# Head pairs that wait for less: new start conditions for the units of an RWKV-7 / mLSTM / mixture-of-experts block, with three key buffers and overlapping token halves

## The chip, the cores and the metric

The kernel runs on one core of a Trainium2 chip. The metric is the device time of one execution in microseconds; lower is better. The time before is the median of three runs, and one more execution was taken with the hardware profiler.

The engines are named as in the profile: PE is TensorE (matmul), PEld its weight loads, DVE is VectorE, ACT is ScalarE, POOL is GpSimd, SP is SyncE, which here issues nearly all DMAs. Each engine works through its own queue in order and waits at semaphores.

## What is computed

One layer of a streaming encoder block on 1024 tokens of width 1024, in float32:

```python
mod = jax.nn.silu(c) @ ada_w[l] + ada_b[l]
sh_m, sc_m, g_m, sh_f, sc_f, g_f = jnp.split(mod, 6, axis=-1)
h = modulate(rms_norm(x, mix_norm_w[l]), sh_m, sc_m)
proj = h @ w_in[l]
y_r = rwkv7_group(proj[..., :RWKV_COLS], ...)    # 8 heads of 64
y_m = mlstm_group(proj[..., RWKV_COLS:], ...)    # 4 heads, keys 64, values 128
y = jnp.concatenate([y_r, y_m], axis=-1) @ w_out[l]
x = x + g_m[:, None, :] * y
h = modulate(rms_norm(x, ffn_norm_w[l]), sh_f, sc_f)
y = hier_moe(h, ...)                             # 32 experts in 4 groups, two per token
x = x + g_f[:, None, :] * y
return rms_norm(x, final_norm_w)
```

The RWKV-7 group is a recurrence over the tokens, for each head with a 64x64 state (decay `w_t`, a rank-one correction `sa b`, a rank-one update `v k`):

```python
def step(state, inp):
    r_t, w_t, k_t, v_t, kk_t, b_t = inp
    sa = jnp.einsum('bhij,bhj->bhi', state, -kk_t)
    state = (state * w_t[:, :, None, :] + sa[..., None] * b_t[:, :, None, :]
             + v_t[..., None] * k_t[:, :, None, :])
    return state, jnp.einsum('bhij,bhj->bhi', state, r_t)
```

The mLSTM group is a chunked linear attention with stabilised exponential gates and a carried matrix state; its output is normalised per head and gated.

## The kernel before

**Stages.** After a short start (the first modulation vectors, four early products) come the mixer, the output projection w_out, the routing and the experts. In the mixer the tokens are in two halves of 512 (`SH`). For each half the normalised input lies transposed in SBUF (`hT`, one buffer), and the columns of `w_in` are taken 128 at a time.

**Jobs.** A `Job` is one such product: 128 columns by 512 tokens, 8 steps over the depth of 1024, each step three matmuls (`mm3`: high by high, high by low, low by high part of split operands), so 24 matmuls of 512 columns into one of two PSUM banks, the lanes. These are the lane matmuls (lines 411 to 413). `fetcher` loads a job's weights (SP, line 425), `splitter` makes the two parts (ACT, then DVE or POOL, lines 440 and 441), `products` issues the matmuls, and the job's `out` reads the lane. A half has one job for the two low-rank inputs `wd` and `ad`, one for `gd`, three per unit (key `k`, receptance `r`, value `v`), twelve for mLSTM and one for its gates. The eight jobs of w_out for each half run through the same lanes (`out_jobs`). `ORDER` is a string per half: a digit stands for the three jobs of that unit, `g` for `gd`, `m` for an mLSTM job.

**Units.** A `Unit` is a pair of RWKV heads in one half: units 0 to 3 in the first, 4 to 7 in the second. Its stages, each a generator:
- `unit_prep`: decays and rates from `wd`, the norm of the keys (`nrm`, a few small DVE steps, then transposed back by PE at line 735), decay-weighted operands `AR` and `BK`, the in-chunk products `G`
- `unit_rest`: transposes the values
- `unit_solve`: inverts 16x16 triangular blocks on DVE. `G` goes to DRAM, is read back as `N16`, the result goes to DRAM as an image and is read back as `X16` and `D16` (SP, line 850; a short D or X in the profile)
- `unit_levels`: puts the blocks together to the 64x64 inverse (PE from line 865)
- `unit_scan`: eight steps in series with the state, each a ping-pong of small matmuls and DVE or POOL operations
- `unit_post`: group norm, bonus, gate, transposition (lines 973 to 998); the result goes to `yTd` in DRAM

**The planner.** PE's order is written out when the kernel is built. `Weave` runs a set of generators in a simulated time. A generator yields a pair (PE time used, latency until it goes on) or a condition; the first ready one in a fixed order of priority is taken, with `products` last, so that lane matmuls fill whatever is left. The latencies stand in the table `LAT`, in microseconds as its author assumed them. A wrong assumption is paid on the chip: PE takes its instructions in that order and stands if an operand isn't there. The other engines' orders come from the compiler's scheduler, with priorities that the generators set.

A unit starts under this condition:

```python
yield lambda: u.jobs[0].done and u.h in b.wd and b.prepped >= n and b.scanned >= n - 1 and b.posted >= n - 1
```

`prepped`, `scanned` and `posted` count the units that have passed the stage: unit n waits until unit n-1 is prepared and unit n-2 is scanned and through post. Keys and receptances have two buffers; their jobs wait for `prepped >= n - 1`.

**The other streams.** `misc` runs in series: the gates of half 0, the remaining four modulation vectors (`ada_rest`, which multiplies rows of `ada_w` into an accumulator on DVE, line 248), `router_x` (64 transposes of x), `h_second` (the second half's `hT`, after all jobs of the first), mLSTM chunks 0 to 3, the gates of half 1, and, once all mLSTM jobs of the half are done, chunks 4 to 7. An mLSTM chunk is 128 tokens: loads, exponentials, scores, numerators (lines 1200 and 1201), the new state (line 1210), and then a tail: norm on ACT and DVE, scaling on POOL, transposition on PE (line 1238), gate, store. `outs` reads y for w_out: the first half's (`y_first`) when all units are prepared and no job of the second half runs, the second half's (`y_second`) after the jobs of w_out's first half. w_out takes its steps over the depth in an order in which unit 7 comes last.

Of the kernel before, what the change touches and what calls it, by code (L numbers as in the profile page):

```python
# [8 lines left out]
F32 = mybir.dt.float32  # L9
# [9 lines left out]
P = 128  # L19
# [19 lines left out]
def f1(n):  # L39
    return n / 2400.0  # L40


LAT = dict(split=3.56, split2=1.5, fetch=4.0, job=1.5, prep0=2.5, prep1=3.06, prep2=11.15, v=0.11, lev1=1.06, lev2=0.35, lev3=1.09, lev4=0.9,
           s1=0.63, s2=0.85, s3=0.51, post1=12.11, post2=5.87, vcm=2.41, gates=20.0, d1=5.0, d2=2.14, d3=0.8, d4=13.0, solve=34.0,
           ada=1.85, x1=18.0, x2=2.5, yk=5.0, lx=2.13, e3=13.7, e4=2.08, rows=12.0, p_prep=-3000, p_rest=0, p_lev=10000, p_scan=300,
           p_post=0, p_gates=0, p_ada=-1000, p_rx=0, p_h=-1000, p_chunk=-1000, p_split=-300, p_prod=0, p_fin=-3000, p_fetch=0, p_y=10000, yk1=1.91,
           u0=0.0)

# [5 lines left out]
class Block:  # L54
# [188 lines left out]
    def ada_k(self, pool, acc, lo, n, tag, bufs, k):  # L243
        nc = self.nc
        a = self.a['ada_w']
        w = pool.tile([P, n], F32, tag=tag + "w", name="ada_w", bufs=bufs)
        nc.sync.dma_start(w, bass.AP(tensor=a.tensor, offset=a.offset + k * P * 6 * D + lo, ap=[[6 * D, P], [1, n]]))
        nc.vector.scalar_tensor_tensor(acc, w, self.csil[:, k:k + 1], acc, op0=ALU.mult, op1=ALU.add)

    def ada_rest(self, pool):  # L250
# [4 lines left out]
        for q in range(4):  # L255
# [4 lines left out]
            for k in range(KD):  # L260
                self.ada_k(pool, acc, lo, D, "adr", 3, k)
                yield 0, LAT['ada']
# [22 lines left out]
    def normed(self, pool, t):  # L285

        nc = self.nc
        j = pool.tile([P, D], BF16, tag="junk", name="junk", bufs=1)
# [74 lines left out]
    def y_first(self, hpool, pool):  # L363
# [3 lines left out]
        for k in self.h_order:  # L367
            t = pool.tile([P, SH], F32, tag="kr"[k % 2], name="yraw", bufs=2)
# [5 lines left out]
    def y_stage(self, pool):  # L374
# [4 lines left out]
        for tag, n in (("k", 2), ("r", 2), ("kk", 1), ("aa", 1), ("cs", 1)):  # L379
            for _ in range(n):  # L380
# [4 lines left out]
                t = self.staged[k] = pool.tile([P, SH], F32, tag=tag, name="yraw", bufs=2 if tag in ("k", "r", "cs") else 1)[:, 0:n_]  # L385
# [83 lines left out]
    def lora_wd(self, pool, h, ps):  # L469
        wd = pool.tile([P, SH], F32, tag="wdad", name="wdad", bufs=2)  # L470
# [4 lines left out]
    def lora_gd(self, pool, h, ps):  # L475
        gd = pool.tile([P, SH], F32, tag="gd", name="gd", bufs=2)
# [104 lines left out]
def products(b):  # L581
# [3 lines left out]
    while b.jobs or b.fetched or b.split or b.running:  # L585
# [8 lines left out]
        for i_, k in enumerate(b.h_order):  # L594
# [8 lines left out]
            yield 3 * f1(512), 0  # L603
# [41 lines left out]
def unit_jobs(u):  # L645
# [4 lines left out]
    def out(name, mu_i):  # L650
        def f(ps):
# [6 lines left out]
            else:  # L658
                t = u.tile(name, [SH], bufs=2)
# [4 lines left out]
    u.jobs = [Job(b, h, 512 + p * P, out("k", 4 + p), when=lambda: b.prepped >= n - 1),  # L664
              Job(b, h, p * P, out("r", p), when=lambda: b.prepped >= n - 1),
# [3 lines left out]
def unit(u):  # L669
    b, n = u.b, u.no  # L670
    w = b.weave
    yield lambda: u.jobs[0].done and u.h in b.wd and b.prepped >= n and b.scanned >= n - 1 and b.posted >= n - 1
# [4 lines left out]
    b.prepped = n + 1  # L677
    t0 = w.now
    yield 'rest'
    yield from unit_rest(u)  # L680
    b.rested = n + 1
    yield lambda: b.levelled >= n
    with b.tc.high_priority(offset=20000):
        unit_solve(u)
# [467 lines left out]
def mlstm_chunk(self, i, pool):  # L1152
# [37 lines left out]
    yield 2 * f32(P), LAT['d3']  # L1190
    C = self.C
    sm = pool.tile([P, 4, 4], F32, tag="msm", name="msm", bufs=2)
    dn, rd, ss, t = (sm[:, j] for j in range(4))
    v4 = lambda x: x.rearrange("p (a e) -> p e a", e=2)
# [11 lines left out]
    if i < NT - 1:  # L1206
# [8 lines left out]
        yield 4 * f32(129), 0  # L1215
    jk = E[:, 0]
# [740 lines left out]
def build(ctx, tc, aps):  # L1957
# [44 lines left out]
    if True:  # L2002
# [4 lines left out]
        for h in range(2):  # L2007
            Job(b, h, 1536, lambda ps, h=h: b.lora_wd(sp, h, ps))
# [3 lines left out]
            for c in ORDER[h]:  # L2012
                if c == "g":
                    Job(b, h, 1536 + P, lambda ps, h=h: b.lora_gd(sp, h, ps))
# [13 lines left out]
        def misc():  # L2028
# [7 lines left out]
            with tc.tile_pool(name="lx", bufs=1, **right) as pool:  # L2036
                yield 'rx'
                yield from router_x(b, pool)
# [3 lines left out]
            with tc.tile_pool(name="at0", bufs=1, **right) as pool:  # L2042
                mlstm_chunks(b, pool)
                for i in range(4):
                    yield 'chunk'
                    yield from mlstm_chunk(b, i, pool)
            misc_done.append(0)
# [4 lines left out]
            with tc.tile_pool(name="at1", bufs=1, **right) as pool:  # L2052
                mlstm_chunks(b, pool)
                for i in range(4, 8):
                    yield 'chunk'
                    yield from mlstm_chunk(b, i, pool)
                misc_done.append(1)
# [66 lines left out]
ORDER = ["0g123mmmmmmmmmmmm", "0gm1mmmmm2mmmmmm3"]  # L2124
# [34 lines left out]
```

## Time and profile before

| | |
|---|---|
| median of 3 runs | 1334.13 us (1328.01 to 1370.47) |
| profiled execution | 1337.15 us |
| its span, first to last instruction | 1335.4 us |
| mean granted TensorE clock | 0.906 |
| PE busy | 1159.8 us, 87% |
| PE weight loads busy | 837.5 us, 63% |
| DVE, ACT, POOL busy | 941.6, 529.5, 389.0 us |

The clock is the share of full speed that the chip granted TensorE, a mean over two levels, 1.0 (2.4 GHz) and 0.5 (1.2 GHz). The span lies inside the profiled execution's own time. Stages by time from the span's start: up to some 62 us the start, then the mixer with its units, from 748.57 us the jobs of w_out, then routing, and the experts from about 945 us to the end.

### The profile page before, as it was taken

What the parts mean: (1) busy time and instruction counts of PE and PEld (TensorE: products, weight loads), DVE (VectorE), ACT (ScalarE), POOL (GpSimd) and SP (SyncE); (2) the same over time, 40 slices, a digit from 0 to 9 for tenths busy, and PEclk for the clock granted to TensorE, in tenths of its full rate; (3) what the DMA queues carried; (4) which work ended last, traced back from release to release, by engine and by line L of the source; (5) the groups of instructions that cost most, each with busy time, mean ns of one, the idle gap of its engine ahead of it and who ended that gap; (6) DMA issues with size and microseconds to landing.
All of it is one profiled execution on the core that took longest, in us unless ns stands there. A gap on an engine that the chain in (4) does not pass through costs nothing. (4 is left out here: it accounts for less than half of the span.)

```text
span 1335.4 us, 21827 instructions
## 1 busy us (share of the span) xinstructions
PE 1159.8 (87%) x7807; PEld 837.5 (63%) x7807; DVE 941.6 (71%) x2024; ACT 529.5 (40%) x1021; POOL 389.0 (29%) x464
## 2 busy tenths in 40 slices
PE   3876889898898998999988799996799998999893
PEld 2654656677566777676756666775566665565553
DVE  6778868876567787757837744743788887777766
ACT  5433222233333442232423332545455655544444
POOL 4613122312232423322324233434222222222212
PEclk8978889878999997999988889879799999999997
DMA  9435545356524443131452454598499989999974
GB/s 318 118 96 164 156 139 183 123 143 189 178 70 99 112 111 79 47 98 49 111 157 70 132 171 123 164 317 282 156 313 318 295 284 295 305 320 332 319 267 170
DMA packets 251935, 246.16 MB, mean 184 GB/s; under 512 B 55064, under 2 KB 190362, under 8 KB 251824
## 3 DMA queue, kind: packets, MB, share of 16 engines
q1 hardware_dynamic: 243504, 228.43, 54.9%
q0 software_dynamic: 8320, 16.31, 5.2%
q8 instruction: 62, 1.02, 0.3%
q14 instruction: 49, 0.40, 0.1%
HBM read 212.13 MB, written 44.74 MB: 192 GB/s over the span
## 5 line engine op out<-in xcount | busy, mean ns | idle before, releaser
L411 PE MATMUL lane<-hTh,whi 128*128 128x512 f32 (+1 forms) x544 | 252.7, 465 | 3.9 <-DVE u L1026 3.5
L412 PE MATMUL lane<-hTl,whi 128*128 128x512 f32 (+1 forms) x544 | 228.0, 419 | 4.2 <-POOL hTl L361 2.6
L413 PE MATMUL lane<-hTh,wlo 128*128 128x512 f32 (+1 forms) x544 | 226.9, 417 | 0.0
L440 ACT CAST whi<-wraw 128x512 fp32r<-128x512 f32 x140 | 84.5, 609 | 267.8 <-PE lane L412 210.0
L441 POOL TENSOR_TENSOR wlo<-wraw,whi 128x512 fp32r<-128x512 f32 (+1 forms) x70 | 92.3, 1320 | 199.9 <-ACT whi L440 173.2
L1667 PE MATMUL yd<-wd,a 128*112 128x512 f32 x256 | 122.0, 615 | 15.8 <-DMA wd<-in_moe_w_down_dram 13.2
L411 PEld LDWEIGHTS lane<-hTh,whi 128*128 128x128 f32 (+1 forms) x544 | 108.9, 200 | 35.8 <-issue 8.0
L413 PEld LDWEIGHTS lane<-hTh,wlo 128*128 128x128 f32 (+1 forms) x544 | 109.3, 201 | 27.6 <-DVE wlo L441 0.3
L412 PEld LDWEIGHTS lane<-hTl,whi 128*128 128x128 f32 (+1 forms) x544 | 110.0, 202 | 22.0 <-POOL hTl L361 3.4
L1590 DVE TENSOR_TENSOR wl<-wa,wh 128x1024 fp32r<-128x1024 f32 x62 | 75.5, 1225 | 40.9 <-ACT wh L1589 39.4
L411 PE MATMUL lane<-wh,xh 128*112 128x512 f32 x256 | 103.8, 405 | 0.0
L413 PE MATMUL lane<-wh,xl 128*112 128x512 f32 x256 | 101.3, 396 | 0.0
L412 PE MATMUL lane<-wl,xh 128*112 128x512 f32 x256 | 101.2, 395 | 0.0
L1694 POOL DMA_INDIRECT x2d<-ys,idx x30 | 44.9, 1496 | 152.8 <-DVE ys L1678 143.9
L1667 PEld LDWEIGHTS yd<-wd,a 128*112 128x112 f32 x256 | 43.9, 184 | 70.7 <-issue 45.1
L1590 DVE TENSOR_TENSOR wl<-wb,wh 128x1024 fp32r<-128x1024 f32 x62 | 76.3, 1230 | 14.0 <-ACT wh L1589 13.8
L1589 ACT CAST wh<-wa 128x1024 fp32r<-128x1024 f32 x64 | 66.8, 1049 | 45.9 <-PE lane L413 17.8
L1589 ACT CAST wh<-wb 128x1024 fp32r<-128x1024 f32 x64 | 67.3, 1051 | 20.1 <-DMA wb<-in_moe_w_up_dram 10.8
L441 DVE TENSOR_TENSOR wlo<-wraw,whi 128x512 fp32r<-128x512 f32 (+1 forms) x70 | 52.3, 747 | 30.3 <-ACT whi L440 17.2
L935 POOL TENSOR_SCALAR sW<-st,WT 128x64 f32<-128x64 f32 x56 | 33.5, 600 | 137.4 <-DVE st L948 118.9
L1596 POOL DMA_INDIRECT xt<-xad,idx x32 | 34.7, 1084 | 121.3 <-PE tp L1620 96.4
L1678 DVE SCALAR_TENSOR_TENSOR ys<-yd,tb,gf 112x512 f32<-112x512 f32 x64 | 44.9, 742 | 14.1 <-PE yd L1667 13.9
(522 smaller groups left out, 2457.8 us busy)
## 6 DMA issues: line engine op xcount, KB each, us to landing
wd<-in_moe_w_down_dram SPq DMA_DIRECT2D x64, 512.0 KB
wraw<-in_w_in_dram SPq DMA_DIRECT2D x104, 256.0 KB
ada_w<-in_ada_w_dram SPq DMA_DIRECT2D x32, 512.0 KB
wa<-in_moe_w_gate_dram SPq DMA_DIRECT2D x32, 512.0 KB
wa<-in_moe_w_up_dram SPq DMA_DIRECT2D x32, 512.0 KB
wb<-in_moe_w_gate_dram SPq DMA_DIRECT2D x32, 512.0 KB
wb<-in_moe_w_up_dram SPq DMA_DIRECT2D x32, 512.0 KB
ada_w<-in_ada_w_dram SPq DMA_DIRECT2D x32, 256.0 KB
```

Source lines behind the costliest of these rows:

```text
L411: nc.tensor.matmul(ps, l[0], r[0], start=first, stop=False)
L412: nc.tensor.matmul(ps, l[0], r[1], start=False, stop=False)
L413: self.mark = nc.tensor.matmul(ps, l[1], r[0], start=False, stop=last)
L440: nc.scalar.copy(hi, raw)
L441: (nc.gpsimd if q else nc.vector).tensor_tensor(lo, raw, hi.bitcast(F32), op=ALU.subtract)
L935: nc.gpsimd.tensor_scalar(sW, st, WT[:, c:c + 1], None, op0=ALU.mult)
L1589: nc.scalar.copy(h, src)
L1590: (engs[n] if engs else nc.vector).tensor_tensor(l, src, h.bitcast(F32), op=ALU.subtract)
L1596: return self.nc.gpsimd.indirect_dma_start(out=self.xts[e % 3], out_offset=None, in_=self.xad[:], in_offset=bass.IndirectOffsetOnAxis(ap=s ...
L1667: self.nc.tensor.matmul(y[:, b], a[:, i], d[:, i, b * 512:b * 512 + 512], start=(i == 0), stop=(i == 1))
L1678: nc.vector.scalar_tensor_tensor(ys[:, bs], py[b], cw, self.gf[0:SL, bs], op0=ALU.mult, op1=ALU.mult)
L1694: self.nc.gpsimd.indirect_dma_start(out=self.x2d[:], out_offset=bass.IndirectOffsetOnAxis(ap=oi, axis=0), in_=ys, in_offset=None, bounds_c ...
```

## The change

- A unit waits for the scan of unit n-2 as before, no longer for its post. The condition on post moves behind `unit_prep`, ahead of `unit_rest`.
- If the levels of unit n-1 are already placed when prep ends, the solve is emitted there, ahead of `unit_rest`; else after the rest, as before, and then the assumed latency of the solve counts from its emission.
- Keys and receptances have three buffers (`KR`), and their jobs wait for `prepped >= n - 2`. To make room, `wdad` and `gd` have one buffer, whose jobs in the second half wait until unit 3 is prepared and through post; the scratch tile of the norm shares a buffer with `hv`. The tiles staged for w_out's second half use the third buffers.
- The planner assumes 4.5 for 3.06 us (norm factors), 28 for 34 (solve), 0.693 for 0.64 us (three lane matmuls).
- `ada_rest` loads and multiplies halves of 512 columns, with six buffers instead of three twice as wide.
- The tail of an mLSTM chunk is a stream of its own, so that the next chunk's loads, exponentials and scores can be placed before it ends. The numerators of chunk i wait until the tail of chunk i-1 is through.
- `router_x` comes after chunks 0 to 3 instead of before `h_second`.
- In the second half all units' jobs come ahead of the mLSTM jobs, as in the first.

```diff
-           ... prep1=3.06 ... solve=34.0,
-           ada=1.85, ...
+           ... prep1=4.5 ... solve=28.0,
+           ada=1.6, ...
+PROD = 0.693
+KR = 3
...
             for k in range(KD):
-                self.ada_k(pool, acc, lo, D, "adr", 3, k)
-                yield 0, LAT['ada']
+                for v in range(2):
+                    self.ada_k(pool, acc[:, v * SH:(v + 1) * SH], lo + v * SH, SH, "adr", 6, k)
+                    yield 0, LAT['ada']
...
-        j = pool.tile([P, D], BF16, tag="junk", name="junk", bufs=1)
+        j = pool.tile([P, SH], F32, tag="hv", name="junk", bufs=1).bitcast(BF16)
...
-            t = pool.tile([P, SH], F32, tag="kr"[k % 2], name="yraw", bufs=2)
+            t = pool.tile([P, SH], F32, tag="kr"[k % 2], name="yraw", bufs=KR)
...
-        for tag, n in (("k", 2), ("r", 2), ("kk", 1), ("aa", 1), ("cs", 1)):
+        for tag, n in (("k", KR), ("r", KR), ("kk", 1)):
...
-        wd = pool.tile([P, SH], F32, tag="wdad", name="wdad", bufs=2)
+        wd = pool.tile([P, SH], F32, tag="wdad", name="wdad", bufs=1)
...
-        gd = pool.tile([P, SH], F32, tag="gd", name="gd", bufs=2)
+        gd = pool.tile([P, SH], F32, tag="gd", name="gd", bufs=1)
...
-            yield 3 * f1(512), 0
+            yield PROD, 0
...
-                t = u.tile(name, [SH], bufs=2)
+                t = u.tile(name, [SH], bufs=KR)
...
-    u.jobs = [Job(b, h, 512 + p * P, out("k", 4 + p), when=lambda: b.prepped >= n - 1),
-              Job(b, h, p * P, out("r", p), when=lambda: b.prepped >= n - 1),
+    u.jobs = [Job(b, h, 512 + p * P, out("k", 4 + p), when=lambda: b.prepped >= n - KR + 1),
+              Job(b, h, p * P, out("r", p), when=lambda: b.prepped >= n - KR + 1),
...
-    yield lambda: u.jobs[0].done and u.h in b.wd and b.prepped >= n and b.scanned >= n - 1 and b.posted >= n - 1
+    yield lambda: u.jobs[0].done and u.h in b.wd and b.prepped >= n and b.scanned >= n - 1
...
     b.prepped = n + 1
+    early = b.levelled >= n
+    if early:
+        with b.tc.high_priority(offset=20000):
+            unit_solve(u)
     t0 = w.now
+    yield lambda: b.posted >= n - 1
     yield 'rest'
     yield from unit_rest(u)
     b.rested = n + 1
-    yield lambda: b.levelled >= n
-    with b.tc.high_priority(offset=20000):
-        unit_solve(u)
+    if not early:
+        yield lambda: b.levelled >= n
+        with b.tc.high_priority(offset=20000):
+            unit_solve(u)
+        t0 = w.now
     yield 0, max(0.0, t0 + LAT['solve'] - w.now)
...
     yield 2 * f32(P), LAT['d3']
+    yield lambda: self.chunks == i
     C = self.C
...
         self.C = Cn
         yield 4 * f32(129), 0
+    self.weave.spawn(mlstm_tail(self, i, pool, E, nv, sm, og))
+
+
+def mlstm_tail(self, i, pool, E, nv, sm, og):
...
+    yield 'chunk'
     jk = E[:, 0]
...
-            Job(b, h, 1536, lambda ps, h=h: b.lora_wd(sp, h, ps))
+            Job(b, h, 1536, lambda ps, h=h: b.lora_wd(sp, h, ps), when=lambda h=h: b.prepped >= 4 * h)
...
-                    Job(b, h, 1536 + P, lambda ps, h=h: b.lora_gd(sp, h, ps))
+                    Job(b, h, 1536 + P, lambda ps, h=h: b.lora_gd(sp, h, ps), when=lambda h=h: b.posted >= 4 * h)
...
-            with tc.tile_pool(name="lx", bufs=1, **right) as pool:
-                yield 'rx'
-                yield from router_x(b, pool)
             with tc.tile_pool(name="h1", bufs=1, **right) as pool:
...
                     yield from mlstm_chunk(b, i, pool)
+                yield lambda: b.chunks == 4
+            with tc.tile_pool(name="lx", bufs=1, **right) as pool:
+                yield 'rx'
+                yield from router_x(b, pool)
             misc_done.append(0)
...
                     yield from mlstm_chunk(b, i, pool)
+                yield lambda: b.chunks == 8
...
-ORDER = ["0g123mmmmmmmmmmmm", "0gm1mmmmm2mmmmmm3"]
+ORDER = ["0g123mmmmmmmmmmmm", "0g123mmmmmmmmmmmm"]
```

## Rows read from the trace of the kernel before

**Rows 1.** The page: busy time of each engine over the span

```profile
PE 1159.8 (87%) x7807; PEld 837.5 (63%) x7807; DVE 941.6 (71%) x2024; ACT 529.5 (40%) x1021; POOL 389.0 (29%) x464
```

**Rows 2.** Stages: window, length, busy us (x) of PE, PEld, DVE, ACT, POOL; clock, DMA

```profile
62.00:849.00 787.00, 695.84 (x5849) 517.34 (x5847) 553.52 (x1438) 257.77 (x567) 227.49 (x299) 0.89 0.44 122
62.00:236.00 174.00, 136.73 (x1173) 101.43 (x1172) 138.03 (x283) 49.07 (x88) 46.50 (x60) 0.84 0.49 145
236.00:405.00 169.00, 152.59 (x1378) 112.68 (x1376) 114.12 (x321) 53.30 (x101) 41.82 (x56) 0.89 0.48 141
540.00:670.00 130.00, 123.03 (x1024) 89.52 (x1023) 95.72 (x256) 44.89 (x89) 37.09 (x59) 0.99 0.32 78
670.00:804.00 134.00, 115.75 (x1035) 85.03 (x1035) 75.62 (x228) 42.69 (x120) 43.39 (x49) 0.85 0.47 132
945.00:1335.00 390.00, 350.08 (x1408) 229.46 (x1408) 300.73 (x365) 199.27 (x285) 89.42 (x67) 0.96 0.88 288
```

**Rows 3.** Timeline of PE around 670: start, us, instruction, [idle before <-releaser]

```profile
668.77 0.39 PE L412 MATMUL lane<-hTl,whi 128*128 128x512 f32 x1
669.00 0.39 PE L413 MATMUL lane<-hTh,wlo 128*128 128x512 f32 x1
674.69 1.08 PE L865 MATMUL tp<-D,G 32*32 32x32 f32 x64 [5.30 <-DMA D<-img]
...
676.29 0.63 PE L412 MATMUL lane<-hTl,whi 128*128 128x512 f32 x1
676.72 0.63 PE L413 MATMUL lane<-hTh,wlo 128*128 128x512 f32 x1
```

**Rows 4.** Waits of PE: who for whom, us in total, times, longest

```profile
PE tp L735 <- DVE nrm L195: 20.1, 4, 12.5
```

**Rows 5.** Timelines of ACT and DVE: units 0, 2 and 7

```profile
171.50 0.69 ACT L449 ACTIVATE k<-lane,omu 128x512 f32<-128x512 f32 x1
...
216.97 0.28 DVE L948 SCALAR_TENSOR_TENSOR stf<-pp,WT,sW 128x64 f32<-128x64 f32 x1
...
243.31 0.59 ACT L998 COPY yt<-tp 128x512 f32<-128x512 f32 x1
249.29 0.69 ACT L711 ACTIVATE sw<-tp,phalf 128x512 f32<-128x512 f32 x1 [5.39 <-PE tp L714]
...
695.93 0.68 ACT L449 ACTIVATE k<-lane,omu 128x512 f32<-128x512 f32 x1
698.35 0.72 ACT L705 ACTIVATE sq<-k,pcol 128x512 f32<-128x512 f32 x1 [1.73 <-POOL k L454]
```

**Rows 6.** Timelines of SP and PE: the solve's reads and unit 7's levels

```profile
667.13 0.54 SPq L850 DMA_DIRECT2D D<-img  x1
...
770.18 0.53 SPq L850 DMA_DIRECT2D D<-img  x1
...
784.80 0.75 PE L865 MATMUL tp<-D,G 32*32 32x32 f32 x64 [0.33 <-DVE pB L1182]
```

**Rows 7.** Timeline of PE: numerators and tails of chunks 4 and 7, lane jobs

```profile
703.19 0.49 PE L1200 MATMUL tp<-vt,pB 128*128 128x129 f32 x2
...
730.62 0.60 PE L1238 MATMUL tp<-ident,mnv 128*128 128x128 f32 x4
...
748.57 0.78 PE L411 MATMUL lane<-hTh,whi 128*128 128x512 f32 x1
...
823.11 0.49 PE L1200 MATMUL tp<-vt,pB 128*128 128x129 f32 x2
...
842.50 0.60 PE L1238 MATMUL tp<-ident,mnv 128*128 128x128 f32 x4
...
849.62 0.47 PE L411 MATMUL lane<-hTh,whi 128*128 128x512 f32 x1
```

**Rows 8.** Lines 248 and 227: ns min/median/max; what DVE waited for

```profile
L248 DVE SCALAR_TENSOR_TENSOR ada_rest<-ada_w,csil,ada_rest x32: 1262/1284/1993, 118.6 to 250.1; 128x1024 f32<-128x1024 f32 x32
...
  DMA ada_w<-in_ada_w_dram: 9.4, 9
...
L227 DVE SCALAR_TENSOR_TENSOR ada_acc<-ada_w,csil,ada_acc x20: 735/750/1750, 19.4 to 48.6; 128x512 f32<-128x512 f32 x20
```

More of the change, by code (lines that the diff above doesn't have):

```diff
@@ L40, in f1 @@
     return n / 2400.0
-LAT = dict(split=3.56, split2=1.5, fetch=4.0, job=1.5, prep0=2.5, prep1=3.06, prep2=11.15, v=0.11, lev1=1.06, lev2=0.35, lev3=1.09, lev4=0.9,
-           s1=0.63, s2=0.85, s3=0.51, post1=12.11, post2=5.87, vcm=2.41, gates=20.0, d1=5.0, d2=2.14, d3=0.8, d4=13.0, solve=34.0,
-           ada=1.85, x1=18.0, x2=2.5, yk=5.0, lx=2.13, e3=13.7, e4=2.08, rows=12.0, p_prep=-3000, p_rest=0, p_lev=10000, p_scan=300,
+LAT = dict(split=3.56, split2=1.5, fetch=4.0, job=1.5, prep0=2.5, prep1=4.5, prep2=11.15, v=0.11, lev1=1.06, lev2=0.35, lev3=1.09, lev4=0.9,
+           s1=0.63, s2=0.85, s3=0.51, post1=12.11, post2=5.87, vcm=2.41, gates=20.0, d1=5.0, d2=2.14, d3=0.8, d4=13.0, solve=28.0,
+           ada=1.6, x1=18.0, x2=2.5, yk=5.0, lx=2.13, e3=13.7, e4=2.08, rows=12.0, p_prep=-3000, p_rest=0, p_lev=10000, p_scan=300,
            p_post=0, p_gates=0, p_ada=-1000, p_rx=0, p_h=-1000, p_chunk=-1000, p_split=-300, p_prod=0, p_fin=-3000, p_fetch=0, p_y=10000, yk1=1.91,
            u0=0.0)
+PROD = 0.693
+KR = 3
 def bcast_rows(ap, n, parts=P):
@@ L384, in y_stage @@
                 n_ = SH if k < 4 else SH - P
-                t = self.staged[k] = pool.tile([P, SH], F32, tag=tag, name="yraw", bufs=2 if tag in ("k", "r", "cs") else 1)[:, 0:n_]
+                t = self.staged[k] = pool.tile([P, SH], F32, tag=tag, name="yraw", bufs=n)[:, 0:n_]
                 self.nc.sync.dma_start(t, self.yTd[k * P:(k + 1) * P, SH:SH + n_])
@@ L1190, in mlstm_chunk @@
     yield 2 * f32(P), LAT['d3']
+    yield lambda: self.chunks == i
     C = self.C
     sm = pool.tile([P, 4, 4], F32, tag="msm", name="msm", bufs=2)
-    dn, rd, ss, t = (sm[:, j] for j in range(4))
-    v4 = lambda x: x.rearrange("p (a e) -> p e a", e=2)
     nv = []
@@ L1215, in mlstm_chunk @@
         yield 4 * f32(129), 0
+    self.weave.spawn(mlstm_tail(self, i, pool, E, nv, sm, og))
+def mlstm_tail(self, i, pool, E, nv, sm, og):
+    nc = self.nc
+    tok = self.tok
+    ts_ = slice(i * P, (i + 1) * P)
+    dn, rd, ss, t = (sm[:, j] for j in range(4))
+    v4 = lambda x: x.rearrange("p (a e) -> p e a", e=2)
+    yield 'chunk'
     jk = E[:, 0]
```

## Prediction

> **What bounds the kernel now.** I read the page's engine line first, then a table of stages, then who waits for whom, then short timelines. TensorE (PE) is busy for 87% of the span, DVE for 71%, ACT and POOL for less [rows 1]. In the table of stages [rows 2] the expert part (945 to 1335) is full and the change does not touch it: whatever the mixer (62 to 849) saves or loses moves that part as a block. In the mixer PE is the bound, but not a full one. Its first row has 695.84 us of busy PE in 787, so 91 us are idle. The granted clock adds to that: a mean of 0.89 between the two levels 1.0 and 0.5 is half speed for 2 x 0.11 of the time, 173 us at 1.2 GHz. A lane matmul (the large product of the input projection) follows the one before it after 0.23 us at 2.4 GHz and after 0.43 us at 1.2 GHz [rows 3], so half speed costs up to half of those 173 us, 87 us. The reader should see two poor stages, 62 to 236 and 670 to 804, and one that shows what is possible, 540 to 670 (7 us idle, clock 0.99). Low clock and gaps go together: the 5.30 us wait that ends at 674.69 is followed by lane matmuls at 0.43 us [rows 3].
>
> The gaps have two kinds of cause. PE runs a fixed order, worked out by a planner that assumes latencies. Where the planner assumed too little, PE stands at the instruction: for the transposed norm factors 20.1 us in 4 waits, the longest 12.5 [rows 4]. And where units start late, the work that could fill the gaps has already been used.
>
> **The change, part by part.** All terms are against the profiled execution: 1337.15 us, of which the span is 1335.4 us; it lies 3 us over the median of the runs, 1334.13.
>
> *The start of a unit.* Unit 0's scan wrote its last state at 216.97, its post copied its result at 243.31, and unit 2's first activation came at 249.29; unit 3 stands to unit 1 in the same way [rows 5]. So the old condition on post is what holds the third unit, by some 26 us, and the new one releases it. It is not the third buffer: the keys of unit 2 were taken out of the lane at 171.50, 78 us before use. In the second half unit 7 starts 2.4 us after its keys come out of the lane (695.93 to 698.35), and so does unit 6; there the order of the jobs holds them, and the third buffer with the new order string releases them. With two interleaved chains of prep, solve, levels and scan, less 26 us for each second unit and without the queue of mLSTM jobs in front of units 6 and 7, I expect the last post some 80 to 120 us earlier than now. No PE work vanishes by this. What it can give is filled gaps. In 670 to 804 idle is 134-115.75 = 18 us and half speed 2 x 0.15 x 134 = 40 us, worth 20: a loss of 38 us; 540 to 670 loses 7+1 = 8 us by the same reckoning [rows 2]. I take 24 of the 30 us between, since those units must now run among others: **-24** (0 to -30). In 236 to 405 the loss is 16+18 = 34 us; I take about half, **-16** (0 to -30).
>
> *The assumed latency of the norm factors* goes from 3.06 to 4.5 us and so puts two more triples of lane matmuls (3 x 0.23 us each) ahead of the transposes, 1.4 us for each of the four waits, and less half speed behind the 12.5 us gap [rows 4]: **-7** (0 to -20).
>
> *The solve* is assumed at 28 us instead of 34, and the lane triple at 0.693 instead of 0.64, so the levels come some 8 us earlier in PE's order. Unit 6's read of the solved blocks was issued at 667.13 and PE had it at 674.69, 7.6 us later; for unit 7 the read was issued at 770.18 and the levels ran at 784.80 [rows 3, 6]. That margin of 7 us is used up by 8 us, and a unit like unit 6, which already waited 5.30 us, waits 13. Behind the waiting level matmuls the whole of PE's queue stands. Bounds 0 (the solve is also emitted earlier, so its reads may come earlier) and +28 (8 us for each of eight units, less half or more that the early start gives); I take **+5**, nearer to the one 5.30 us wait on record.
>
> *The mLSTM tail* becomes a stream of its own, and the next chunk's loads, exponentials and score matmuls run beside it. But the numerators of chunk i+1 still wait for the last transpose of chunk i. In the second half the first numerators start at 703.19 and the fourth chunk's at 823.11, a period of 40 us; the tail's transposes follow 27 us (730.62) and 19 us (842.50) later [rows 7]. That part, 23 us in the mean, stays serial. These four chunks now come last, after all jobs of the half, and w_out's second half needs them. Cover is w_out's first half, which took 748.57 to 849.62 with the last scan in it [rows 7]; of its 101 us 8 jobs x 24 x 0.23 = 44 us are lanes, and I estimate 90 without the scan. The chain is some 14 us of loads and four periods of 23+1: 110 us. Of the 20 us uncovered I take **+8**, since the tail's engines will be freer (bounds 0 and +75, below). On SP the next chunk's load of the gate rows now waits for the squares of the tail, with weight loads of w_out queued behind it; these are fetched a job ahead, which hides it; with that cover gone a job of 5.5 us would stand, once per chunk, 16 us for the three.
>
> *The first read of y for w_out* waits until the last job of the half. In the old order unit 7's products ran in the gap between the tail's transposes at 730.62 and the first lane matmul at 748.57 [rows 7]; now only a chunk's few do: **+3** (0 to +14).
>
> *The modulation weights* come in 64 pieces of 512 columns. A 1024-wide step takes 1284 ns and a 512-wide one 750 ns [rows 8], so DVE does 64 x 0.750 - 32 x 1.284 = 7 us more, between 118 and 250 or later. DVE is free for 174-138 = 36 us of 62 to 236 [rows 2], which hides it; without that cover the 7 us would count. The norm factors' small steps, which queue between such steps, get through sooner. SP issues 32 more, past weight loads and the solve's reads, at about the 0.5 us of its other issues [rows 6]: 16 us of a queue that has room. I take 0 (-3 to +8). The Trainium skill, "DMA: Bandwidth & Descriptors" (Anatomy of one DMA), speaks against such splits: some 2 us fixed for each DMA, an estimate of 64 us more in all if loads came one by one. With six buffers in flight that would not show, and the trace has only 9.4 us of DVE waits for these loads with three buffers [rows 8]; by that page's figure, with loads one by one, the sum would be some 60 us higher. I give that no chance.
>
> *One buffer for the low-rank tiles, the scratch tile shared with the norm, router transposes after the chunks* I take at nothing: the new conditions on the low-rank jobs of the second half (prep and post of unit 3 done) come true as early as the units do, and the transposes only move to a time when lanes are plentiful. Held up, a job costs its 5.5 us.
>
> Sum: -24-16-7+5+8+3 = -31 us, 1337.15 - 31 = 1306; on the level of the median, 3 us lower, **1303**.
>
> **The rivals.**
>
> *The order changes nothing* (1325 to 1345, at 1331). PE has lane jobs from 748.57 on without a break [rows 7], and the order before spreads the units among them so that unit 7's latency is covered. If the stalls come from planned against real latencies, tighter ones (0.693, 28) give back what the overlap brings: the -47 of the three gains shrinks to a third, -16, and +16 stands against it. For it: of 91 us of gaps one line's four waits hold 20 [rows 4], and the rest is scattered. Against: two poor stages with the clock at 0.84 and 0.85 [rows 2].
>
> *More than that* (1245 to 1285, at 1266). Busy matmul time hides slack: a lane matmul counts as 0.39 us though the next starts after 0.23 [rows 3]. Measured by weight loads, PEld is busy 0.69 of 540 to 670, but 0.58 of 62 to 236, 0.67 of 236 to 405 and 0.63 of 670 to 804 [rows 2]; at 0.69 the three would shrink by 27, 6 and 11 us, and two fifths of the (56+37+40)/2 = 66 us that half speed costs in these stages with them, 27 more: 71 us. The Trainium skill, "Perfetto Trace Analysis" (Identifying the Most-Contended Engine), says the same of matmul busy time and wants weight loads read instead; the rows bear it out. Against: the start (62 to 236) hangs on DVE and loads, which the change barely helps.
>
> *The chunks' chain is left bare: slower* (1345 to 1390, at 1374). If the split tail does not shorten the period, because DVE, ACT and POOL order the tail behind the next chunk's work, four chunks take 14+4x40 = 174 us against 90 of cover; with 5 us of that gone because w_out's second half can do three of its eight steps in two lanes first, 79 us are bare instead of 8: 1303+71 = 1374. It decides above a period of 30 us (slower than before) and 37 us (by over 2%). For it: the period was 40 with the same instructions; against: 19 us are the shortest serial part [rows 7].
>
> **How the numbers follow.** Forecast (1284 to 1322) 0.46; nothing changes 0.24; more 0.16; the bare chain 0.14. What this kernel's measurement can tell from no change is about 2%: 1307 and 1361. Of the forecast's case 0.29 lies below 1307, so faster is 0.29+0.16 = 0.45; of the bare chain 0.12 lies over 1361: slower 0.12 and the same 0.43. The range runs from 1262, inside the case of more, to 1345, the upper end of no change; it leaves out the slower case and the lowest ends.
>
> **What would show it.** Unit 2 starting near 220; the last post before 780; no wait above 5 us before the transposed norm factors; levels waiting for the solve's reads (the +5) in more than one unit; a chunk period near 25 us and a gap of PE before w_out's second half of about 8 us; clock in the stage before w_out above 0.95. I am wrong if the last post comes early and PE still stands, with low clock, in the chunks' stage, or if the waits for the solve add up to more than 15 us.

## The result: 4.1% slower, and where the mixer loses it

The changed kernel takes 1390.2 us (median of 4 runs, 1377.89 to 1390.75) against 1331.8 us for the kernel before on the same chip (median of 4, 1328.01 to 1370.47): a ratio of 1.041 with a 95% interval of 1.036 to 1.046. In some executions this chip runs a kernel some per cent slower, and the ratios here leave these out, as that of 1370.47 us. The forecast was 1303 with a range of 1262 to 1345, so the sign was wrong and the time is outside the range. The profiled execution took 1390.75 us, its span 1389.0 us, with a mean clock of 0.892 (before 0.906).

First the page's engine line of the changed kernel, then its table of stages (columns as in [rows 2]).

```profile
PE 1171.9 (84%) x7807; PEld 846.7 (61%) x7807; DVE 931.9 (67%) x2056; ACT 530.6 (38%) x1021; POOL 385.6 (28%) x464
```

```profile
62.00:236.00 174.00, 132.94 (x1164) 96.03 (x1163) 131.46 (x304) 49.19 (x88) 42.29 (x62) 0.83 0.40 115
236.00:405.00 169.00, 145.55 (x1329) 106.88 (x1327) 115.00 (x327) 42.67 (x81) 39.77 (x54) 0.87 0.41 118
...
540.00:670.00 130.00, 110.89 (x965) 82.18 (x965) 80.61 (x243) 36.94 (x67) 29.91 (x48) 0.83 0.41 114
670.00:804.00 134.00, 119.23 (x1082) 86.98 (x1080) 70.81 (x174) 47.02 (x86) 35.38 (x39) 0.91 0.41 111
...
789.00:908.00 119.00, 103.11 (x590) 78.75 (x588) 56.49 (x175) 40.86 (x144) 42.18 (x46) 0.84 0.49 143
...
1000.00:1389.00 389.00, 349.90 (x1408) 229.56 (x1408) 298.21 (x364) 199.57 (x285) 87.03 (x66) 0.96 0.88 287
```

PE still has 7807 matmuls [rows 1], and the experts still take 389 us (390 in [rows 2]). So nearly the whole loss lies between 62 us and the first expert matmul, at 948 us before and 1000 us after. That stretch in the kernel before and in the changed one:

```profile
62.00:948.00 886.00, 773.63 (x6246) 579.17 (x6244) 600.97 (x1568) 301.38 (x690) 269.19 (x352) 0.88 0.47 136
```

```profile
62.00:1000.00 938.00, 786.56 (x6245) 589.18 (x6244) 591.36 (x1600) 301.75 (x689) 265.28 (x352) 0.86 0.45 129
```

It is 52 us longer. Idle PE time (length less busy PE) is 886 - 773.6 = 112 us before and 938 - 786.6 = 151 us after, 39 us more; the other 13 us are busy time of the same matmuls. The clock has a part in this: by the clock records of the two traces, PE ran at half speed (1.2 GHz) for 206 us of the stretch before and for 254 us after. That is 48 us more, and a microsecond at half speed costs up to half of one, so up to 24.

By the prediction's reckoning of a stage (idle time, and the clock's shortfall times the length), 670 to 804 lost 38 us before and loses 15 + 12 = 27 now. But 236 to 405 loses 23 + 22 = 45 us instead of 34, and 540 to 670, the stage that had shown what is possible, 19 + 22 = 41 instead of 8. The units did move into it, and they took their gaps along.

PE's waits in the changed kernel, in the form of [rows 4], show who was late:

```profile
PE tp L748 <- DVE nrm L199: 38.1, 6, 14.0
PE pr L940 <- DVE st L961: 21.4, 16, 6.3
PE pu L951 <- DVE R L943: 16.9, 12, 3.8
...
PE pp L958 <- DVE UV L954: 7.8, 7, 3.3
```

Before, the first was 20.1 us [rows 4]; the next three, all of the scan, were these:

```profile
PE pu L938 <- DVE R L930: 9.7, 9, 4.1
...
PE pr L927 <- DVE st L948: 5.3, 8, 1.8
...
PE pp L945 <- DVE UV L941: 5.0, 3, 3.7
```

These four lines grew by 44 us, about as much as the idle time. All are waits for VectorE, whose busy time didn't grow. Not its amount of work but the order in its queue is in question. Its timeline ahead of the 7.78 us wait for unit 7's norm factors:

```profile
646.96 0.15 DVE L733 TENSOR_SCALAR nrm<-tp 128x8 f32<-128x8 f32 x1
647.03 0.38 DVE L850 TENSOR_TENSOR Xt<-N,XD 64x121 f32<-64x121 f32 x1
...
650.46 1.22 DVE L199 SCALAR_TENSOR_TENSOR gvr<-nrs 128x8 f32<-128x8 f32 x1
651.61 0.15 DVE L197 SCALAR_TENSOR_TENSOR nrs<-nrs 128x8 f32<-128x8 f32 x1
651.69 0.31 DVE L852 TENSOR_REDUCE XD<-Xt 64x13 f32<-64x169 f32 x1
651.92 0.67 DVE L991 TENSOR_TENSOR Y<-Y,gvr 128x512 f32<-128x512 f32 x1
652.52 0.15 DVE L198 TENSOR_TENSOR nrs<-nrs,nrm 128x8 f32<-128x8 f32 x1
652.60 0.47 DVE L850 TENSOR_TENSOR Xt<-N,XD 64x196 f32<-64x196 f32 x1
653.00 0.67 DVE L998 TENSOR_TENSOR Y<-Y,gn 128x512 f32<-128x512 f32 x1
653.60 0.15 DVE L199 SCALAR_TENSOR_TENSOR nrs<-nrs 128x8 f32<-128x8 f32 x1
...
657.80 0.15 DVE L199 SCALAR_TENSOR_TENSOR nrm<-nrs 128x8 f32<-128x8 f32 x1
```

```profile
658.10 1.97 PE L748 MATMUL tp<-ident,nrm 128*64 128x128 f32 x16 [7.78 <-DVE nrm L199]
```

The chain of unit 7's norm factors is eleven steps, most of them of 0.15 us (nrm to nrm). Between them stand the solve of unit 6 (`Xt`, `XD`), the post of unit 5 (`Y`, `gvr`) and, in the lines left out, the reading of an mLSTM job's lane and a split of weights. From its first to its last step it took 11.0 us with 36 DVE instructions, its own included; before, unit 7's took 4.1 us with 15. Over the eight units these chains sum to 38 us before and 63 us after, and the eight scans, from first to last matmul, to 335 and 358 us. Units that overlap on PE interleave on VectorE, and PE, whose order is fixed, stands for that.

What PE did before one fall of the clock is seen in three adjoining windows of the changed kernel, first for all instructions, then for those of the lanes alone:

```profile
745.50:789.30 43.80, 43.79 (x412) 34.87 (x411) 13.70 (x32) 16.32 (x34) 11.42 (x11) 1.00 0.45 133
789.30:793.30 4.00, 1.73 (x29) 1.21 (x28) 3.08 (x7) 3.98 (x8) 2.57 (x2) 1.00 0.11 27
793.30:820.60 27.30, 24.23 (x124) 16.82 (x124) 8.48 (x30) 4.70 (x16) 8.04 (x10) 0.50 0.46 138
```

```profile
745.50:789.30 43.80, 38.60 (x156) 28.00 (x154) 0.75 (x1) 3.63 (x6) 1.00 0.45 133
789.30:793.30 4.00, 0.02 (x1) 0.00 (x0) 0.00 (x0) 0.30 (x1) 1.00 0.11 27
793.30:820.60 27.30, 9.13 (x18) 5.34 (x18) 0.00 (x0) 0.29 (x1) 0.50 0.46 138
```

After 156 lane matmuls in 44 us come 4 us with one, in which only a scan runs and PE is busy for 1.73 us; then the clock is 0.50 for 27 us. Over the mixer the clock fell 26 times before and 31 times after.

### The profile page after: what moved, and what is told of

It is laid out like the page before. It is cut to its first block, busy times and chain, and to the rows that moved or that the text cites. A ratio compares the mean times of both kernels' runs of the same rounds, so it can differ in the third digit from the quotient of the medians.

```text
span 1389.0 us, 21961 instructions
## 1 busy us (share of the span) xinstructions
PE 1171.9 (84%) x7807; PEld 846.7 (61%) x7807; DVE 931.9 (67%) x2056; ACT 530.6 (38%) x1021; POOL 385.6 (28%) x464
## 4 chain that ended last, share of the span: by engine, by line
PE 46%; DMA 24%; DVE 19%; issue 4%; ACT 2%; SPq 2%; POOL 1%; DVEq 0%; ACTq 0%; POOLq 0%
PE lane L417 9%; PE lane L418 8%; PE lane L419 7%; PE yd L1690 4%; DMA wd<-in_moe_w_down_dram 4%; DMA ada_w<-in_ada_w_dram 3%; DMA wb<-in_moe_w_gate_dram 3%; DMA wa<-in_moe_w_up_dram 3%; DMA pB<-rowd 2%; DMA wa<-in_moe_w_gate_dram 2%; DMA wb<-in_moe_w_up_dram 2%; PE tp L774 2%; DVE ada_rest L253 2%; DVE Xt L850 1%; DMA wiB<-rowd 1%
## 5 line engine op out<-in xcount | busy, mean ns | idle before, releaser
L446 ACT CAST whi<-wraw 128x512 fp32r<-128x512 f32 (+1 forms) x140 | 84.7, 609 | 290.6 <-PE lane L418 234.9
L447 POOL TENSOR_TENSOR wlo<-wraw,whi 128x512 fp32r<-128x512 f32 x70 | 95.5, 1364 | 222.1 <-ACT whi L446 218.8
L253 DVE SCALAR_TENSOR_TENSOR ada_rest<-ada_w,csil,ada_rest 128x512 f32<-128x512 f32 x64 | 47.2, 768 | 13.6 <-DMA ada_w<-in_ada_w_dram 12.9
```

The source lines that it names most:

```text
L446: nc.scalar.copy(hi, raw)
L447: (nc.gpsimd if q else nc.vector).tensor_tensor(lo, raw, hi.bitcast(F32), op=ALU.subtract)
```

## The experiments

The theories that the expectations name: **T1** the planner's 0.693 us for a lane triple; **T2** the order string; **T3** the shorter solve and the other assumed latencies; **T4** PE's order before is a searched-out one, and any shift costs (how that order came about, no run shows); **T5** the structure (overlap of units) costs whatever is assumed; **T6** the value job paces the units; **T7** overlapped units make DVE steps later than assumed, and PE stands for that. The table gives medians, the ratio to before with its interval, and PE's idle and half-speed time from 62 us to the first expert matmul, counted as above (the expectations have 108 and 147 us for the idle time before and after). Each of the last two columns is of one profiled execution. By the clock recorded with every run, the time at 1.2 GHz over the whole span (2 x (1 - clock) x span) lies between 211 and 273 us in 47 runs of the kernel before alone, so differences of some 30 us in the last column tell nothing.

| run | median us | ratio to before | idle | half speed |
|---|---|---|---|---|
| before | 1331.8 to 1339.7 on six occasions | 1 | 112 | 206 |
| after | 1390.2 | 1.041 (1.036 to 1.046) | 151 | 254 |
| a_prod | 1392.2 | 1.045 (1.038 to 1.052) | 139 | 262 |
| a_order | 1385.6 | 1.038 (1.032 to 1.045) | 151 | 258 |
| a_lat | 1383.9 | 1.039 (1.032 to 1.046) | 153 | 248 |
| a_latprod | 1384.2 | 1.039 (1.032 to 1.046) | 152 | 270 |
| b_prod | 1369.2 | 1.028 (1.021 to 1.035) | 136 | 230 |
| n1_ada | 1338.6 | 1.006 (1.002 to 1.010) | 117 | 197 |
| n2_post1 | 1355.9 | 1.021 (1.015 to 1.027) | 118 | 230 |
| n3_x1 | 1332.7 | 1.001 (0.997 to 1.005) | 110 | 180 |
| b_start | 1371.5 | 1.030 (1.021 to 1.040) | 137 | 238 |
| b_v2 | 1362.3 | 1.021 (1.016 to 1.027) | 127 | 238 |
| b_start_v2 | 1388.1 | 1.037 (1.031 to 1.044) | 136 | 300 |
| a_v2r2 | 1399.0 | 1.049 (1.043 to 1.054) | 160 | 279 |
| b_tail | 1344.0 | 1.006 (1.002 to 1.009) | 122 | 190 |
| a_post | 1397.8 | 1.048 (1.040 to 1.056) | 148 | 279 |
| a_scan | 1378.3 | 1.032 (1.023 to 1.041) | 156 | 228 |
| a_nrm | 1372.6 | 1.026 (1.017 to 1.034) | 122 | 279 |
| a_nrmscan | 1372.7 | 1.025 (1.020 to 1.030) | 149 | 227 |
| b_nrm | 1376.0 | 1.030 (1.024 to 1.037) | 133 | 266 |

**The planner's numbers and the order.** a_prod, a_order, a_lat and a_latprod are the changed kernel with one thing put back; b_prod is the kernel before with the new triple.

```diff
a_prod     -PROD = 0.693                       +PROD = 0.64
a_order    -"0g123mmmmmmmmmmmm"  (half 1)      +"0gm1mmmmm2mmmmmm3"
a_lat      -prep1=4.5 solve=28.0 ada=1.6       +prep1=3.06 solve=34.0 ada=1.85
a_latprod  both a_prod and a_lat
b_prod     -yield 3 * f1(512), 0               +yield 0.693, 0
```

> The changed kernel with one number set back: the planner counts 0.64 us for three lane matmuls again, not 0.693. Theory of the clock of the planner (T1): 0.693 puts 8% fewer lane matmuls under every assumed latency, so PE stands at short steps (the scan's state 21.4 us against 5.3 before, R 16.9 against 9.7, norm factors 38.1 against 20.1) and falls to half speed behind them; set back, these waits fall to near those of before and the time to about 1355, at least 25 us below the changed kernel. Theory of the order (T2): the units-first order of the second half and the bare end make the loss; then this changes less than 12 us either way.

> The changed kernel with the old order of jobs in the second half (units spread among the mLSTM jobs). T2 (order): the last lane job of the half ends near 735 again instead of 789 and the time is at or below 1345. T1 (planner's clock): the waits of PE for state, R and norm factors stay as in the changed kernel, the time stays within 12 us of 1390.

> The changed kernel with the three old latencies (3.06 for the norm factors, 34 for the solve, 1.85 for a modulation step). If the shorter solve costs (T3, the term of the prediction that I took at +5): the waits before the levels vanish and the time falls by 10 us or more, but the norm-factor waits grow. T1 and T2 both expect less than 10 us of difference.

> The kernel before with one number changed: 0.693 us for three lane matmuls. T1: waits of PE for state, R and norm factors rise by 25 us or more in sum and the time by 20 us or more over before. T2: within 10 us of before. A change of either sign that large would also show how much any shift of PE's order moves the time.

> The whole new structure with all four planner numbers of before (0.64, 3.06, 34, 1.85). T1: the loss was in the numbers, so 1350 or less. T4: one more order that nobody searched for: 1360 to 1400, near the other variants of the changed kernel. T5: 1375 or more, since the structure is still there.

All four variants of the changed kernel lie within 0.7% of each other: neither the numbers nor the order string is the cause by itself (T1 to T3 fall). The order string alone does nothing, though with the old one PE waits 19.2 us for the solved blocks. Yet 0.693 alone costs the kernel before 2.8%.

**Shifts that change nothing else.** One assumed latency of the kernel before is moved by a trifle, so that PE's order differs and nothing more.

```diff
n1_ada    -ada=1.85     +ada=1.80
n2_post1  -post1=12.11  +post1=12.5
n3_x1     -x1=18.0      +x1=17.0
```

> The kernel before with the assumed latency of a modulation step at 1.80 instead of 1.85 us, which no chip resource feels: only PE's fixed order shifts. Theory of the tuned order (T4): the order before is a lucky or searched-out one, and nearly any shift of it costs; the time is 15 to 45 us over before. Theory of the planner's clock (T1): 0.693 costs by shortening the cover of each latency, a thing that this edit leaves alone; within 8 us of before. T5 (the new structure itself costs, whatever the order): within 8 us of before too.

> The kernel before with the assumed latency of the first step of post at 12.5 instead of 12.11 us: a second shift of the order without meaning. T4: 15 to 45 us over before, by another amount than the first. T1 and T5: within 8 us of before.

> The kernel before with one planner number moved by a trifle (the assumed latency of the first step of the second half's input, 18 to 17 us): the third shift of PE's order that changes nothing else. The two others cost 0.6% and 2.1%. T4 (the order before is a searched-out one, any shift costs): 1336 to 1360. Rival (the 2.1% was an exception): within 0.3% of before, 1328 to 1336.

They cost 0.6%, 2.1% and 0.1%. T4 holds in part: of the nine variants of the kernel before in this study none is faster, and a shift alone can cost 2%, but need not cost anything. A single part that costs 2 to 3% alone can therefore not be told from a shift by its time.

**The units' start, the values, the tail.**

```diff
b_start     (before)  - ... and b.scanned >= n - 1 and b.posted >= n - 1
                      + ... and b.scanned >= n - 1
                      + yield lambda: b.posted >= n - 1    # ahead of 'rest'
b_v2        (before)  + two buffers of v, its job waits for b.rested >= n - 1; one of wdad and gd
b_start_v2  (before)  both
a_v2r2      (after)   + two buffers of v, as above; two of r instead of three
b_tail      (before)  + the tail of a chunk as a stream of its own
a_post      (after)   + the old start condition, with b.posted >= n - 1
```

> The kernel before with the start condition alone: the wait for post of unit n-2 goes behind prep, the solve and everything else stay. My prediction's step: units 2 and 3 start some 26 us earlier and the time falls by up to 16 us. Theory of the value chain (T6: rest n waits for the value job of unit n, which may only start after rest n-1, so rest and levels keep their period of some 85 us): the third unit's prep comes earlier, its scan does not, and the time does not fall. T4: 15 to 45 us over before by the shift alone.

> The kernel before with a second buffer for the values, whose job then waits for rest n-2 instead of rest n-1 (paid with single buffers for the low-rank tiles, as in the change). T6 (the value job paces the units): rest of units 1 to 3 comes earlier, but in this kernel the start condition on post still holds the third unit, so the gain is small: 1325 to 1345. T4 (any shift of the order costs): 1340 to 1370 with no unit earlier.

> The start condition of the change and a second value buffer together, all else as before. T6: with the pacing job gone the start condition now bites: rest and levels of units 2 and 3 come 25 us or more earlier than in the run with the start condition alone (286 and 365 for rest there), the last post too, and the time is below that run's 1371 by 15 us or more. If the units come earlier and the time does not fall, PE's density and not the units' period sets the time (T5).

> The changed kernel with two buffers of values and two of receptances instead of one and three. T6: rest of unit 7 comes before 700 instead of at 750, its scan ends before 780 instead of at 834, and the time falls by 15 us or more below 1390. T5: the units come earlier, idle time and half speed stay, and so does the time, within 12 us.

> The kernel before with the tail of the mLSTM chunk as a stream of its own, nothing else. My prediction: the chunk period falls from 37 us to about 25 where it is not held by other things; alone it gives 0 to -10 us, since the chunks hide under w_out's jobs. T4: 5 to 40 us over before.

> The changed kernel with the old start condition put back (unit n also waits for the post of unit n-2 before prep); the third buffers, the order string, the split tail and the planner's numbers stay. T5 (the overlap of the units by the start condition is the dear part; it cost 3.0% alone): most of it comes back, 1345 to 1365. Rival (the other parts cost as much by themselves): 1380 to 1395.

T6 is right about the units and wrong about the time. In the changed kernel the rests of units 4 to 7 begin at 493, 581, 682 and 750 us, each behind its values, which have one buffer; unit 7's leave the lane at 748.58. With two buffers of values the last post (line 1011) comes 57 us earlier, at 808.50 instead of 865.29, and the kernel is no faster, 1399 us:

```profile
808.50 0.59 ACT L1011 COPY yt<-tp 128x512 f32<-128x512 f32 x1 [1.41 <-PE tp L1009]
```

So it isn't the lateness of the units that costs. The costs don't add either: 3.0% and 2.1% alone are 3.7% together, and the start condition, 3.0% alone, gives nothing back when it is taken out of the changed kernel. That was a miss of mine: T5 in the form "the start condition is the dear part" falls.

a_post also shows what the overlap does and what it doesn't. With the old start condition back, unit 7's chain of norm factors takes 4.2 us with 11 DVE instructions (11.0 in the changed kernel), and unit 3's 4.4 instead of 10.4 us. So the overlap is what lengthened these chains. But the time doesn't fall with them. PE still waits 30 us for norm factors, since unit 2's chain now takes 16.5 us with 14 modulation steps in it:

```profile
PE tp L748 <- DVE nrm L199: 30.2, 5, 14.6
```

Nor do the four waits together rank the kernels by time: they are 61 us in a_post and a_prod (1398 and 1392 us), 84 in the changed kernel (1390) and 89 in a_latprod (1384).

**The waits for VectorE.** The planner is told longer latencies where PE waits, so that its order has lane matmuls there.

```diff
a_nrm      (after)   -prep1=4.5                  +prep1=10.0
a_scan     (after)   -s1=0.63, s2=0.85, s3=0.51  +s1=1.3, s2=1.5, s3=0.9
a_nrmscan  (after)   both
b_nrm      (before)  -prep1=3.06                 +prep1=10.0
```

> The changed kernel with one difference: the planner assumes the steps of the scan to take 1.3, 1.5 and 0.9 us instead of 0.63, 0.85 and 0.51, so PE's order has more lane matmuls between the small matmuls of a scan. Nothing of the computation changes. In the changed kernel PE waits 21.4 us for the scan's new state, 16.9 for R and 7.8 for UV, against 5.3, 9.7 and 5.0 before. T7 (the overlap makes the scan's DVE steps later than planned, and PE stands for that): these three waits shrink from 46 to under 20 us, and the time falls by 15 to 25 us, to 1363 to 1376. T5 (the overlap costs whatever the planner assumes: what is saved at one place is lost at another): the three waits shrink and others grow, 1380 to 1395. T4 (any shift moves the time by 7 to 25 us): either, with no relation to these waits.

> The changed kernel with one difference: the planner assumes 10 us instead of 4.5 for the norm factors. Nothing of the computation changes. PE waits 38.1 us in 6 waits for the transposed norm factors (longest 14.0) in the changed kernel. T7, the same for the prep (its DVE steps queue behind those of the unit it overlaps): those waits fall by 5.5 us each, to about 10 us, and the time by 15 to 28 us, to 1360 to 1375. T5: other waits grow by as much, 1380 to 1395.

> The changed kernel with both longer assumptions: 10 us for the norm factors and 1.3, 1.5 and 0.9 us for the scan's steps. Nothing of the computation changes. Alone they gave 1372.6 and 1378.3 against 1390.2. T7 (PE's waits for late DVE steps are what the overlap costs, and planned at their real length they are filled): the two gains add up, 1355 to 1365, and idle time of the mixer falls from 147 to about 110 us. T5 (what is saved as idle time is lost as half speed or elsewhere): no better than the better one alone, 1368 to 1385, with idle time down and half speed up, as for the norm factors alone (idle 147 to 117, half speed 254 to 278 us).

> The kernel before with one difference: 10 us instead of 3.06 for the norm factors, where PE waits 20.1 us in 4 waits. Nothing of the computation changes. If those waits are plain loss, which a longer assumption fills with lane matmuls, as in the changed kernel: 1315 to 1325, faster than both kernels. T4 (the order before is a searched-out one in which the later transposes also delay the units): 1335 to 1360.

Three of these kernels by PE's waits, a_nrm, a_nrmscan and b_nrm in turn:

```profile
PE pr L940 <- DVE st L961: 12.8, 7, 5.3
...
PE tp L748 <- DVE nrm L199: 9.1, 2, 8.2
PE pu L951 <- DVE R L943: 8.9, 9, 3.3
```

```profile
PE tp L878 <- DMA D<-img: 24.2, 3, 16.3
PE tp L748 <- DVE nrm L199: 18.5, 3, 7.4
```

```profile
PE pr L927 <- DVE st L948: 14.5, 10, 2.5
...
PE pp L945 <- DVE UV L941: 11.3, 6, 5.1
...
PE tp L735 <- DVE nrm L195: 6.9, 1, 6.9
```

In a_nrm the wait falls from 38.1 to 9.1 us, idle time by 30 us, and the ratio from 1.041 to 1.026; half speed rises by 25 us in the profiled execution, the longest of its four. In a_scan the three waits of the scan fall from 46 to 28 us, not under 20 as expected, and it gains 0.9 points, a gain that its interval doesn't separate from nothing. Both together give no more than the first alone: now PE stands 24.2 us for the solve's blocks, which it did for 1.2 us in the changed kernel. In the kernel before the same longer number takes the wait down just as well, from 20.1 to 6.9 us, and costs 3.0%: the scan's waits and half speed (266 against 206 us) take its place. So T7 is right for one wait of the changed kernel and not for the rest. The 1.5 points that a_nrm gains go with that wait, but the longer number also shifts PE's order everywhere, and by the time alone the two can't be told apart. No version here beats the kernel before.

## Why the prediction was wrong, step by step

*The start of a unit (-24 and -16).* The start itself came as forecast: unit 2's first activation, at 249.29 us before [rows 5], is at 212.63.

```profile
212.63 0.69 ACT L724 ACTIVATE sw<-tp,phalf 128x512 f32<-128x512 f32 x1 [2.00 <-PE tp L727]
...
748.58 0.68 ACT L455 ACTIVATE v<-lane,omu 128x512 f32<-128x512 f32 x1
...
865.29 0.57 ACT L1011 COPY yt<-tp 128x512 f32<-128x512 f32 x1
```

Two steps behind it failed. "The last post some 80 to 120 us earlier" overlooked the value job: keys and receptances got a third buffer, values kept one, and a unit's rest waits for them. The last post came at 865 us, not earlier than before:

```profile
858.38 0.59 ACT L998 COPY yt<-tp 128x512 f32<-128x512 f32 x1 [5.23 <-PE tp L996]
```

And "what it can give is filled gaps" is the step that failed in kind: a_v2r2, in which the units do come early, is with a_post the slowest kernel of all. Of the 24 us expected in 670 to 804 some 11 came; 236 to 405 lost 11 us instead of gaining 16, and 540 to 670 lost 33. An overlapped unit brings no lane matmuls to fill gaps with, only more small DVE steps into one queue, and its own gaps. I had priced the stages 236 to 405 and 670 to 804 as idle time waiting for work. In the kernel before, PE's waits for VectorE make 14 of the 16 us idle in the first, and 12 of the 18 in the second, where another 5.30 are the solve's read [rows 3].

*The norm factors (-7).* The wait grew from 20.1 to 38.1 us instead of falling. The 4.5 us assumed were right for a lone chain (4.1 us for unit 7 before, 4.2 in a_post) and wrong for one that overlaps (11.0 us).

*The solve (+5).* Levels waited 1.2 us for its reads, before 5.30 [rows 3]: the earlier emission covers the shorter assumption, the lower bound of the term. The margin is spent in a_nrmscan and a_order.

*The chunks (+8).* Right in mechanism. PE's numerators and tail transposes:

```profile
808.20 0.80 PE L1212 MATMUL tp<-vt,pB 128*128 128x129 f32 x2
...
835.62 0.66 PE L1261 MATMUL tp<-ident,mnv 128*128 128x128 f32 x4
836.12 0.39 PE L1212 MATMUL tp<-vt,pB 128*128 128x129 f32 x2
...
859.42 0.60 PE L1261 MATMUL tp<-ident,mnv 128*128 128x128 f32 x4
859.86 0.39 PE L1212 MATMUL tp<-vt,pB 128*128 128x129 f32 x2
...
901.44 0.60 PE L1261 MATMUL tp<-ident,mnv 128*128 128x128 f32 x4
```

The period (from one chunk's numerators to the next's) is 28 us, then 24, under the 30 from which the bare-chain rival decides; that rival gave 1374, nearest to the result, but by a mechanism that didn't occur, so its nearness is luck. w_out's second half starts at 908, 7 us behind the last tail, with two waits of 1 us. That the first half of w_out took 111 us (797 to 908) and not the 90 of the estimate is the step's miss: the last scan still ran in it, in a stage with 16 us idle and a clock of 0.84 (789 to 908). b_tail shows that the split alone gains nothing (+0.6%).

*The first read of y (+3).* PE had no lane job from 789.3 to 797.1 us and stood for 4 us of that, as forecast in size; the 27 us at half speed behind it, shown above, were not in the term.

*The modulation weights (0).* 64 pieces of 743 ns (median), DVE waits 12.9 us for them instead of 9.4 [rows 8]. The fixed cost of some 2 us for each DMA that the Trainium skill states in "DMA: Bandwidth & Descriptors" (Anatomy of one DMA) is given there for DMAs issued from GpSimd, while SP issues these; the estimate of 60 us from it, for loads one by one, has no place in that row. The steps end at 356 us instead of 250. The norm factors' steps didn't get through sooner between the smaller pieces: unit 1's chain took 15.1 us with twelve of them in it, before 13.5 with six. This part, the router's move, the early solve, the third buffers of keys and receptances, and the single low-rank buffers by themselves were not run.

```profile
L253 DVE SCALAR_TENSOR_TENSOR ada_rest<-ada_w,csil,ada_rest x64: 716/743/1755, 115.4 to 355.8; 128x512 f32<-128x512 f32 x64
...
  DMA ada_w<-in_ada_w_dram: 12.9, 4
```

*The block behind* held: the experts take 389 us. *The rivals:* "tighter latencies give back what the overlap brings" had the right place, PE's fixed order against real latencies, but I priced it as a lost gain, never as a loss. What I took as evidence against it, two poor stages, was its evidence. (Its own figures, -16 and +16, give 1334 and not 1331.) *The signs:* unit 2 near 220 and the chunks' period near 25 came true; the last post before 780 and no wait above 5 us for the norm factors (14.0) did not.

What is shown: the loss lies in the mixer, 39 us as idle PE time and 13 us as longer busy time of the same matmuls; PE's waits at VectorE's steps grew by 44 us; the overlap lengthens the chains of the units that it touches (unit 7's 11.0 us, 4.2 with the old start condition). What is not shown is that this lengthening costs the time: a_post takes it away for units 3 and 7 and gives nothing back, and only a_nrm, which plans for one of the waits, gives 1.5 points. So the cause of the 4.1% stays open: how much belongs to the parts that were not run alone, and how much to PE's order being another one than before. Three shifts without content cost 0.1 to 2.1%, so a large share of either would fit, and a search of the changed kernel's planner numbers, which would tell, was not made.

## What to carry to other kernels

Before overlapping more chains to fill an engine's gaps, see who ends the gaps: if it is another engine's queue, a second chain can lengthen the first one's latency there (4.2 to 11.0 us here), and PE's fixed order turns that into a wait. Where an order is written out from assumed latencies, measure what a shift without content costs (here up to 2.1%) before giving a part's cost to the part. And when a start condition is relaxed, follow every operand of the next stage: the one left with a single buffer sets the pace (here that of the units, though not the time).

## What the runs showed of the hardware that was not expected

Filling a gap did not mend the clock. In b_nrm PE's wait for the norm factors fell from 20.1 to 6.9 us, and yet the granted clock of its four runs is 0.873 to 0.887, against 0.898 to 0.906 in seven runs of the kernel before on the same chip. By the sum above the table that is 328 us at 1.2 GHz in the mean against 261, worth up to 33 of the 36 us by which b_nrm is slower. a_post, whose four waits are 24 us shorter than the changed kernel's, has 0.873 to 0.886 in its four runs, the changed kernel 0.890 to 0.898. So an order with fewer or shorter waits can spend more time at half speed, and what a change of PE's order does to the clock has to be read from several runs: the runs of one kernel, the one before, differ by up to 62 us in it.
